# Softmax weights of the C heads turned by VectorE and DRAM instead of TensorE, with the convolution's taps spread over more steps, in a one-layer hybrid decoder block

## The chip, the cores and the metric

One core of a Trainium2 chip runs the whole program. The metric is the device time of one execution in microseconds (us), and of several executions the median. A profiled execution is one more execution, recorded by the hardware profiler. Its times in the trace count from the start of its span. Engines are called PE (TensorE), DVE (VectorE), ACT (ScalarE), POOL (GpSimd) and SP (SyncE, which here only issues DMAs).

## The reference

One layer on 512 tokens of width 2048, in float32, cut to what matters:

```
h   = rms_norm(x)
p   = h @ W_in                       # split by columns: A q k v | B u g | C q k v
A:  8 heads x 64, dilated sliding windows (128,1), (512,4), (2048,16)
B:  glu(u, g) -> causal depthwise conv, 31 taps, 512 channels -> layer norm -> swish
C:  16 query heads x 64 on 2 k/v heads, window 128, a sink per head
        w = exp(s - m) ; o = (w @ v) / (sum(w) + exp(sink - m))
x   = x + concat(A, B, C) @ W_out
x   = x + swiglu(rms_norm(x))        # width 5632
```

Attention of a C head is banded: a block of 128 queries sees its own block of keys and the one before it. For `w @ v` on PE, w must lie with keys in the partitions, while scores and softmax leave it with queries in the partitions. So each C head's weights, 128 x 512 in four packed blocks of 128 x 128, must be transposed.

## The kernel before, in words

Everything is kept with channels in partitions and the 512 tokens as columns. Each float32 operand is split in a high and a low half that PE multiplies at full rate, and each product is three matmuls of 128 x 512 (`mm3`, L322 high by high, L323 low activations by high weights, L324 high activations by low weights). The halves of the weights are made per unit of 1024 weight columns: ACT casts `wh` (L289), DVE subtracts `wl` (L263, in the FFN L285). SP loads the raw tile `w` (L243).

The program has these stages in a row on PE: idle matmuls that bridge the first loads (L348); the first four projection blocks together (`in`, the first 12 matmuls of them at L516, from four small weight tiles); 26 more projection blocks (`project`), each 2 units of weights; 32 half blocks of the output projection (`o`, two PSUM banks by turns, each freed by the residual add at L1098 on DVE); the FFN's two big products with a seven-product scheme (`out`, L1304 to L1307 up, L1569 to L1571 down); and a short end with one turn of a leftover piece (`sides`, L1534).

The mixers A, B and C run underneath the projection's matmuls. What they issue on every engine is put in order by hand, by a clock of ticks: `ticks.after(n, fn)` runs `fn` n ticks later, and `project` ticks once for every two of its k steps, that is after every 6 matmuls. Each engine then works its instructions in that order, waiting at each for its inputs. SP's queue is in order too: a DMA that waits for its source holds back the loads behind it.

For a head of C (`head(h)` in `attention`), the steps are: `scores` (PE L843/L844, tile `c3s` for mixer c3), `pack` (DVE), `packed_exps` (ACT, tile `c0e`), `packed_norm` (DVE L870, sums and their reciprocals), then `packed_flip`: four PE transposes (L877) into a PSUM bank `c0t`. One tick later `packed_high` casts the high half (ACT L883, `c0hp`), then `packed_low` subtracts for the low half (DVE L888, `c0lp`), `spread_out` masks both for the two key blocks (POOL L897/L900, `c0ph`, `c0pl`), and `weigh` multiplies by v (PE L965/L966, `c0o`). `C_TICKS` holds the distances; its seventh entry `fl` is the ticks from `packed_norm` to the flip. `at_v` adds them up to place `weigh`.

The values v are already turned on another path (`do_v`): DVE turns 32 x 32 blocks (L747), four DMAs write them to DRAM so that the blocks change places (L753, 32 x 16 x 32 with runs of 128 bytes), and one DMA reads the result back (L759).

The convolution of B is 124 DVE operations (`tap`: 4 of form L571, 120 of form L573, each on up to 128 x 512). Tap number i of block j comes `TAP_TICKS[j]` ticks after the one before; the last falls on tick 193, and the layer norm starts by tick 246.

Of the kernel before, what the change touches and what calls it, by code (L numbers as in the profile page):

```python
# [9 lines left out]
F32 = mybir.dt.float32  # L10
# [3 lines left out]
AF = mybir.ActivationFunctionType  # L14
# [17 lines left out]

OUT_ORDER = (list(range(16)), [n + o for n in range(6) for o in (0, 8)] + [6, 7, 14, 15])

TAP_TICKS = (1.2, 1.3, 1.6, 1.6)
T_LN = 244
T_GLU = 14

# [1 line left out]
SD, KD, VD, EV = 9, 6, 12, 1  # L40


C_TICKS = (1, 6, 2, 2, 2, 3, 5, 1, 4)
A_TICKS = (0, 8, 2, 1, 3, 1, 3, 1, 5)


# [70 lines left out]
def kernel(ctx: ExitStack, tc: tile.TileContext, xT, wi, wo, wgu, wd, cst_in, outT):  # L117
# [20 lines left out]
    def slot(name, dt=F32, cols=T):  # L138
        return sp.tile([P, cols], dt, name=name, tag="s")

    def bank(name, cols=T, pool="banks"):
        return psum[pool].tile([P, cols], F32, name=name, tag="b")
# [114 lines left out]
    def lows_now():  # L257
        if lows and cooling:
            release()
            pump(RAW_EARLY if at["use"] <= 20 else RAW_BUFS)  # L260
        while lows:
            fn, *args = lows.pop(0)
            fn(*args)  # L263
        if late_lows and not cooling:
            pump(RAW_EARLY if at["use"] <= 20 else RAW_BUFS)

    def split_up_to(i):
        while at["split"] <= min(i, len(works) - 1):
            key, last, eng = works[at["split"]]
            of = [b for b, k in held.items() if k == key]  # L270
            t, n = drop(key) if last else raws[key]
            if cooling:
                held.update((b, None) for b in of)
                cool.extend(of)
            u = at["split"]
            hi = wp.tile([P, 1024], F32R, name=f"wh{u}", tag="hi", bufs=SPLIT_BUFS)
            lo = wp.tile([P, 1024], F32R, name=f"wl{u}", tag="lo", bufs=SPLIT_BUFS)
            if eng == "moves":

                near = psum["high"].tile([P, 1024], F32R, name=f"wn{u}", tag="h")  # L280
                src = t[:, :n].rearrange("p (n f c) -> p f n c", n=4, c=P)
                by = lambda x: x[:, :n].rearrange("p (f n c) -> p f n c", n=4, c=P)
                nc.scalar.copy(by(near), src)
                nc.scalar.copy(by(hi), src)
                nc.vector.tensor_sub(by(lo), src, by(near).bitcast(F32))  # L285
            elif eng or "high" not in psum:
                eng = eng or nc.vector

                (nc.vector.tensor_copy if u == 0 else nc.scalar.copy)(hi[:, :n], t[:, :n])  # L289
                lows.append((eng.tensor_sub, lo[:, :n], t[:, :n], hi[:, :n].bitcast(F32)))  # L290
                if not late_lows:
                    lows_now()
            else:
                near = psum["high"].tile([P, 1024], F32R, name=f"wn{u}", tag="h")
                nc.scalar.copy(near[:, :n], t[:, :n])
                nc.scalar.copy(hi[:, :n], t[:, :n])
                lows.append((nc.vector.tensor_sub, lo[:, :n], t[:, :n], near[:, :n].bitcast(F32)))
                if not late_lows:
                    lows_now()
            splits[u] = (hi, lo)  # L300
            at["split"] += 1
# [44 lines left out]
    b = bank("idle")  # L346
    for i in range(WARM):
        nc.tensor.matmul(b, idle, idle[:, None, :].to_broadcast([P, NT, P]), start=True, stop=True)  # L348
    b = idle = None

    nhalf = cp.tile([P, 8], F32, name="nhalf")
# [6 lines left out]
    def col(i):  # L358
        return cst[:, i:i + 1]
# [39 lines left out]

    def scaled(x, g, tag, k):  # L400
        hi, lo = slot(f"{tag}h{k}", F32R), slot(f"{tag}l{k}", F32R)
        nc.scalar.activation(hi, x, AF.Copy, scale=g)
        nc.vector.scalar_tensor_tensor(lo, x, g, hi.bitcast(F32), op0=ALU.mult, op1=ALU.subtract)
        return hi, lo

# [71 lines left out]

    g4 = [bank(f"in{j}") for j in range(HEAD4)]
    h_hl = {}
    split_up_to(0)  # L480
    h_hl[0] = scaled(xs[0], col(C_G1), "h", 0)
    split_up_to(1)
    h_hl[1] = scaled(xs[1], col(C_G1 + 1), "h", 1)
    split_up_to(2)
    pump(RAW_EARLY)
    for k in range(KT):

        if k == 1:
            split_up_to(3)
        if k + 2 < KT:  # L490
            h_hl[k + 2] = scaled(xs[k + 2], col(C_G1 + k + 2), "h", k + 2)
        if k == 0:

            at["use"] = 2
            first = [splits.pop(u) for u in range(2)]
        elif k < 4 or k % 2 == 0:
            wh, wl = next_unit()
            o = 0
        if k + X_AHEAD < KT:
            load_first(k + X_AHEAD)  # L500
        elif k + X_AHEAD == KT:

            nc.sync.dma_start(cst[:, C_G2:], cst_in[:, C_G2:])
        if k == 0:
            add_square(ssum, xs[0], 0, "sq")
        if k + 1 < KT:
            add_square(ssum, xs[k + 1], k + 1, "sq")
        hi, lo = h_hl.pop(k)
        h_hi.append(hi)
        h_lo.append(lo)  # L510
        if k == 0:

            for part, u in ((0, 0), (0, 1), (2, 0), (1, 0), (1, 1), (2, 1)):
                for j in range(2):
                    w = first[u][part == 2][:, j * P:(j + 1) * P]
                    nc.tensor.matmul(g4[2 * u + j], w, (hi, lo, hi)[part], start=part == 0, stop=False)  # L516
            first = w = None
            continue
        for j in range(HEAD4):
            mm3(g4[j], wh[:, o:o + P], wl[:, o:o + P], hi, lo, False, k == KT - 1)  # L520
            o += P
# [274 lines left out]
    def attention(kind, box, mix, mi, heads):  # L796
# [34 lines left out]
        def head(h):  # L831
# [38 lines left out]
                nc.vector.tensor_add(den, den, mx)  # L870
                invert(h, den)

            def packed_flip():
                b = bank(f"{name}t{h}")
                for i in range(NT):
                    s = slice(i * P, (i + 1) * P)
                    nc.tensor.transpose(b[:, s], es["e"][:, s], ident)  # L877
                es.clear()
                ticks.after(ev, packed_high, b)

            def packed_high(b):
                hi = slot(f"{name}hp{h}", F32R)
# [114 lines left out]
            if kind == "c":  # L997
                ticks.after(tu, packed_exps)
                ticks.after(tu + s2, packed_norm)
                ticks.after(tu + s2 + fl, packed_flip)  # L1000
            else:
                for t in range(len(TBANKS[kind])):
                    ticks.after(tu + s2 + fl + t, flip, t)
# [213 lines left out]
    def later(n, fn, *args, queue=evacs):  # L1217
        while len(queue) <= n:
            queue.append([])
        queue[n].append((fn, *args))  # L1220
# [250 lines left out]
    def turn_back(key, lo=0, hi=T):  # L1471

        g, i, k, a = key
        if (g, i, k) not in pairs_out:
            name, c = BACK[g, i, k]
            pairs_out[g, i, k] = wp.tile([P, 1024], F32, name=f"z{g}{i}{k}", tag=f"raw{final_bufs[c][name]}", bufs=1)
        z = pairs_out[g, i, k].rearrange("p (b a j) -> p a b j", a=2, j=32)[:, a, lo // 32:hi // 32]
        nc.vector.transpose(z, y[key][:, lo:hi].rearrange("p (b j) -> p b j", j=32))
        if hi == T:
            y.pop(key)  # L1480
# [10 lines left out]
    class Down:  # L1491
# [100 lines left out]
        def copy_u(self, a, b):  # L1592
            u = slot(f"d{self.t}u{a}")
            nc.scalar.copy(u, b)
            later(0, self.less, 1, 0, a, u, nc.gpsimd)

        def done(self, q, banks):
            for a, b in enumerate(banks):
                if q == 7:
                    self.add(1, 1, a, b)  # L1600
                elif q == 1:
                    self.add(0, 0, a, b)
                elif q == 4:
                    self.add(1, 0, a, b)
                elif q == 6:
                    if a:
                        later(0, self.six, a, b)
                    else:
                        self.six(a, b)
                elif q == 5:  # L1610
                    self.less(1, 1, a, b)
                    if self.end:
                        turn_back(self.sum(1, 1, a))
                        if a == 1:
                            t = y[self.sum(0, 1, a)][:, TH:]
                            nc.vector.tensor_add(t, t, b[:, TH:])
                            later(0, put, self.g, 1, 1)
                else:
                    self.add(0, q - 2, a, b)
            if self.end and q == 6:  # L1620
                for a in range(2):
                    later(a, turn_back, self.sum(1, 0, a))
                later(2, put, self.g, 1, 0, queue=extras)
            if q == 3 and self.final:
                for n, (i, k) in enumerate(((0, 0), (1, 1), (1, 0), (0, 1))):
                    for a in range(2):
                        later((2, 3, 6, 7)[n] + a, turn_back, self.sum(i, k, a))
                    later((4, 5, 8, 9)[n], put, self.g, i, k, queue=extras)
# [90 lines left out]
```

## Time and profile before

| | us |
|---|---|
| median of 3 runs | 1841.1 |
| the three runs | 1840.91, 1841.10, 1842.79 |
| profiled execution, its own time | 1842.92 |
| its span in the trace | 1841.2 |

The profiled execution stands 1.8 us above the median, and 1.7 us of its time lie outside its span. The granted clock of PE over the span is 1.000. To read the stages: the first four projection blocks end at about 51 us, the projection and the mixers run to about 387 us, the output projection to 578 us, and from there to the end the FFN. A page of the profile gives for each engine the busy time, a chain of work that ended last, and the idle time before groups of instructions with the engine that ended it; views of the trace give the same by window, tile or time.

### The profile page before, as it was taken

The page shows a single profiled execution, that of the slowest core. Times are in us where ns is not written, and L with a number is a line of the kernel's source. Part 1 is how long each engine was busy: PE and PEld are TensorE (multiplying, and loading weights), DVE is VectorE, ACT ScalarE, POOL GpSimd, SP SyncE. Part 2 cuts the span into 40 slices and gives each one's busy share as a digit, 9 for nine tenths or more (in the row PEclk, how much of TensorE's full clock was granted, in tenths as well). Part 3 has the DMA queues.
Part 4 walks back from the last instruction along what each step waited for, and adds up shares of the span by engine and source line. Part 5 has one row for each costly group of instructions (what it writes and reads, how often), then busy time and mean ns, then how long its engine had stood idle before and what let it go on. Part 6 is the DMA issues. An engine that isn't in the chain of part 4 may idle for free.

```text
span 1841.2 us, 26561 instructions
## 1 busy us (share of the span) xinstructions
PE 1834.3 (100%) x8314; PEld 1522.9 (83%) x8314; DVE 1429.5 (78%) x2023; ACT 1313.2 (71%) x1784; POOL 1019.3 (55%) x793
## 2 busy tenths in 40 slices
PE   9999999999999999999999999999999999999998
PEld 7888888888888888888888888888888888888887
DVE  6689888986689877778777787777777777777777
ACT  6355644553468788888888888888887778777775
POOL 0126544110003557876878767887776559776552
PEclk9999999999999999999999999999999999999999
DMA  7354245363343456777867777677687579777635
GB/s 276 87 150 119 90 133 162 110 168 130 132 139 103 115 157 186 196 206 187 226 181 208 203 190 223 176 209 210 175 272 256 202 230 300 245 260 259 238 120 109
DMA packets 401613, 337.81 MB, mean 183 GB/s; under 512 B 185409, under 2 KB 327873, under 8 KB 401473
## 3 DMA queue, kind: packets, MB, share of 16 engines
q1 hardware_dynamic: 400896, 335.33, 62.6%
q8 instruction: 66, 1.08, 0.2%
q10 hardware_dynamic: 576, 0.79, 0.1%
q14 instruction: 75, 0.61, 0.1%
HBM read 261.61 MB, written 66.03 MB: 178 GB/s over the span
## 4 chain that ended last, share of the span: by engine, by line
PE 99%; DVE 1%; DMA 0%; issue 0%; ACT 0%; SPq 0%; DVEq 0%; ACTq 0%
PE out L1307 15%; PE out L1306 15%; PE out L1304 15%; PE out L1569 7%; PE out L1570 7%; PE out L1571 7%; PE o L322 3%; PE o L324 3%; PE o L323 3%; PE cq L322 2%; PE cq L323 2%; PE cq L324 2%; PE aq L322 1%; PE ak L322 1%; PE aq L324 1%; PE av L322 1%
## 5 line engine op out<-in xcount | busy, mean ns | idle before, releaser
L1307 PE MATMUL out<-wh,h 128*128 128x512 f32 x1232 | 479.3, 389 | 0.0
L1306 PE MATMUL out<-wl,h 128*128 128x512 f32 x1232 | 479.3, 389 | 0.0
L1304 PE MATMUL out<-wh,h 128*128 128x512 f32 x1232 | 479.3, 389 | 0.0
L1306 PEld LDWEIGHTS out<-wl,h 128*128 128x128 f32 x1232 | 231.2, 188 | 48.1
L1304 PEld LDWEIGHTS out<-wh,h 128*128 128x128 f32 x1232 | 231.2, 188 | 48.0
L1307 PEld LDWEIGHTS out<-wh,h 128*128 128x128 f32 x1232 | 231.2, 188 | 47.9
L1570 PE MATMUL out<-wl,a 128*128 128x512 f32 x620 | 240.5, 388 | 0.1
L1569 PE MATMUL out<-wh,a 128*128 128x512 f32 x620 | 240.4, 388 | 0.0
L1571 PE MATMUL out<-wh,a 128*128 128x512 f32 x620 | 240.4, 388 | 0.0
L289 ACT CAST wh<-w 128x1024 fp32r<-128x1024 f32 (+2 forms) x94 | 97.0, 1031 | 139.4 <-PE o L323 49.9
L1579 DVE TENSOR_TENSOR y<-y,out 128x512 f32<-128x512 f32 x192 | 128.5, 683 | 48.1 <-PE out L1571 46.8
L263 DVE TENSOR_TENSOR wl<-w,wh 128x1024 fp32r<-128x1024 f32 (+2 forms) x95 | 114.4, 1204 | 34.8 <-ACT wh L289 34.6
L1570 PEld LDWEIGHTS out<-wl,a 128*128 128x128 f32 x620 | 116.4, 188 | 24.2 <-DVE wl L285 0.5
L1571 PEld LDWEIGHTS out<-wh,a 128*128 128x128 f32 x620 | 116.4, 188 | 23.9
L1569 PEld LDWEIGHTS out<-wh,a 128*128 128x128 f32 x620 | 116.4, 188 | 23.9
L573 DVE SCALAR_TENSOR_TENSOR y<-bu,cst,y 128x511 f32<-128x511 f32 (+14 forms) x120 | 88.8, 740 | 1.1
L322 PE MATMUL o<-mh_c,wh 128*128 128x512 f32 x128 | 51.0, 399 | 0.0
L322 PE MATMUL cq<-hh,wh 128*128 128x512 f32 x128 | 50.3, 393 | 0.0
L324 PE MATMUL o<-mh_c,wl 128*128 128x512 f32 x128 | 50.0, 391 | 0.0
L323 PE MATMUL o<-ml_c,wh 128*128 128x512 f32 x128 | 50.0, 390 | 0.0
L323 PE MATMUL cq<-hl,wh 128*128 128x512 f32 x128 | 49.9, 390 | 0.0
L324 PE MATMUL cq<-hh,wl 128*128 128x512 f32 x128 | 49.9, 390 | 0.0
(2353 smaller groups left out, 4746.8 us busy)
## 6 DMA issues: line engine op xcount, KB each, us to landing
od<-a SPq DMA_DIRECT2D x154, 256.0 KB
a<-od SPq DMA_DIRECT2D x154, 256.0 KB
w<-in_wi SPq DMA_DIRECT2D x58, 512.0 KB
w<-in_wo SPq DMA_DIRECT2D x32, 512.0 KB
x<-in_xT SPq DMA_DIRECT2D x16, 256.0 KB
xr<-in_xT SPq DMA_DIRECT2D x16, 256.0 KB
x2d<-xr SPq DMA_DIRECT2D x16, 256.0 KB
z<-x2d SPq DMA_DIRECT2D x64, 64.0 KB
```

What stands on the lines that cost most here:

```text
L263: fn(*args)
L289: (nc.vector.tensor_copy if u == 0 else nc.scalar.copy)(hi[:, :n], t[:, :n])
L322: nc.tensor.matmul(out, wh, xh, start=start, stop=False)
L323: nc.tensor.matmul(out, wh, xl, start=False, stop=False)
L324: nc.tensor.matmul(out, wl, xh, start=False, stop=stop)
L1304: nc.tensor.matmul(b, x[:, high], wh[:, s], start=c == f == 0 and q in (7, 1, 5, 2), stop=False, skip_group_check=True)
L1306: nc.tensor.matmul(b, x[:, high], wl[:, s], start=False, stop=False, skip_group_check=True)
L1307: nc.tensor.matmul(b, x[:, low], wh[:, s], start=False, stop=c == f == 1, skip_group_check=True)
L1569: nc.tensor.matmul(b[:, lo:hi], x[:, high], wh[:, s], start=start, stop=False, skip_group_check=True)
L1570: nc.tensor.matmul(b[:, lo:hi], x[:, high], wl[:, s], start=False, stop=False, skip_group_check=True)
L1571: nc.tensor.matmul(b[:, lo:hi], x[:, low], wh[:, s], start=False, stop=last, skip_group_check=True)
L1579: getattr(eng, op)(t, t, src)
```

## The change

For the C heads, `packed_flip` is gone. `packed_turn` runs right behind `packed_norm`: DVE turns the 32 x 32 blocks of the weights (`c0z`). One tick later four SP DMAs write it to DRAM (`c0ed`), two ticks later one SP DMA reads it back into SBUF (`c0et`), and four ticks after that `packed_high` and `packed_low` work from `c0et` in SBUF in place of `c0t` in PSUM. `fl` grows from 5 to 6, so that `packed_high` and all behind it, `weigh` too, comes one tick later.

The taps' distances grow, and the last tap falls on tick 224 in place of 193, 31 later. The layer norm's tick stays.

At the start there are five more small idle matmuls; the cast of the first activation tile (`hh`) is shared by ACT and DVE; the low half of the first weight units is made after the low half of that tile; and the first 12 matmuls go high-high, low-high, then high-low for all.

At the end of the FFN, the evacuation of the second bank of product 5 (`five`) is put off to the next turn of the queue of evacuations.

```diff
-TAP_TICKS = (1.2, 1.3, 1.6, 1.6)
+TAP_TICKS = (1.4, 1.5, 1.9, 1.9)
-C_TICKS = (1, 6, 2, 2, 2, 3, 5, 1, 4)
+C_TICKS = (1, 6, 2, 2, 2, 3, 6, 1, 4)
...
+    for i in range(5):
+        nc.tensor.matmul(b[:, :P], idle, idle, start=True, stop=True)
...
-        nc.scalar.activation(hi, x, AF.Copy, scale=g)
+        if k or tag != "h":
+            nc.scalar.activation(hi, x, AF.Copy, scale=g)
+        else:
+            nc.scalar.activation(hi[:, :TH], x[:, :TH], AF.Copy, scale=g)
+            nc.vector.tensor_scalar(hi[:, TH:], x[:, TH:], g, None, op0=ALU.mult)
...
+    late_lows.append(True)
     split_up_to(0)
     h_hl[0] = scaled(xs[0], col(C_G1), "h", 0)
+    lows_now()
+    late_lows.clear()
...
-            for part, u in ((0, 0), (0, 1), (2, 0), (1, 0), (1, 1), (2, 1)):
+            for part, u in ((0, 0), (0, 1), (1, 0), (1, 1), (2, 0), (2, 1)):
...
-            def packed_flip():
-                b = bank(f"{name}t{h}")
-                for i in range(NT):
-                    s = slice(i * P, (i + 1) * P)
-                    nc.tensor.transpose(b[:, s], es["e"][:, s], ident)
-                es.clear()
-                ticks.after(ev, packed_high, b)
+            def packed_turn():
+                z = slot(f"{name}z{h}")
+                nc.vector.transpose(z, es.pop("e"))
+                ticks.after(1, packed_leave, z)
+            def packed_leave(z):
+                d = tc.dram_tile([T, P], F32, name=f"{name}ed{h}")
+                for a in range(4):
+                    at = slice(32 * a, 32 * a + 32)
+                    nc.sync.dma_start(d.rearrange("(n i) c -> i n c", i=32)[:, :, at],
+                                      z[at].rearrange("p (n c) -> p n c", c=32))
+                ticks.after(2, packed_back, d)
+            def packed_back(d):
+                t = slot(f"{name}et{h}")
+                nc.sync.dma_start(t.rearrange("p (b c) -> p b c", b=NT), d.rearrange("(b p) c -> p b c", p=P))
+                ticks.after(fl + ev - 3, packed_high, t)
...
-                ticks.after(tu + s2 + fl, packed_flip)
+                ticks.after(tu + s2, packed_turn)
...
+        def five(self, a, b):
+            self.less(1, 1, a, b)
+            if self.end:
+                turn_back(self.sum(1, 1, a))
+                ...
                 elif q == 5:
-                    self.less(1, 1, a, b)
-                    if self.end:
-                        turn_back(self.sum(1, 1, a))
-                        ...
+                    if self.end and a:
+                        later(0, self.five, a, b)
+                    else:
+                        self.five(a, b)
```

Three places show how it moves instructions. The first is PE at the flip of mixer c0's head 0, between the end of projection block `cq` and the scores of c3. Before:

```order
L324 MATMUL cq_1138<-hh_479,wl_1082 128x512
L877 MATMUL c0t_1252<-ident,c0e_1120 128x128 x4
L843 MATMUL c3s_1260<-ckh_1000,cq_1014 128x256
L844 MATMUL c3s_1260<-ckl_1001,cq_1014 128x256
L843 MATMUL c3s_1260<-ckh_1000,cq_1014 128x256
L844 MATMUL c3s_1260<-ckl_1001,cq_1014 128x256
L322 MATMUL bu_1272<-hh_142,wh_1139 128x512
```

After the change:

```order
L324 MATMUL cq_1140<-hh_485,wl_1085 128x512
L852 MATMUL c3s_1264<-ckh_1004,cq_1018 128x256
L853 MATMUL c3s_1264<-ckl_1005,cq_1018 128x256
L852 MATMUL c3s_1264<-ckh_1004,cq_1018 128x256
L853 MATMUL c3s_1264<-ckl_1005,cq_1018 128x256
L322 MATMUL bu_1276<-hh_146,wh_1141 128x512
```

The transposes are gone and nothing takes their place on PE.

The second place is SP's queue around the same two heads (`w` are weight loads, `cq1d` to `cq1t` the trip of a query block's norms, `c0sums` that of the heads' sums). Before:

```order
L243 DMA w_1155<-in_wi 128x1024
L642 DMA cq1d<-cq1p 32x4x4 x4
L685 DMA cq_1133<-cq1l 64x512
L686 DMA cq_1134<-cq1l 64x512
L243 DMA w_1220<-in_wi 128x1024
L647 DMA cq1t<-cq1d 128x16
L243 DMA w_1293<-in_wi 128x1024
L816 DMA c0sums<-weights_sums_553 8x32 x4
```

After the change:

```order
L243 DMA w_1157<-in_wi 128x1024
L892 DMA c0ed_1201<-c0z_1186 32x16x32 x4
L651 DMA cq1d<-cq1p 32x4x4 x4
L694 DMA cq_1135<-cq1l 64x512
L695 DMA cq_1136<-cq1l 64x512
L243 DMA w_1229<-in_wi 128x1024
L898 DMA c0et_1244<-c0ed_1201 128x4x128
L656 DMA cq1t<-cq1d 128x16
L243 DMA w_1298<-in_wi 128x1024
L825 DMA c0sums<-weights_sums_559 8x32 x4
L892 DMA c0ed_1321<-c0z_1290 32x16x32 x4
L898 DMA c0et_1362<-c0ed_1321 128x4x128
```

Head 0's write stands ahead of the query block's trip and its read between two weight loads; head 1's write and read stand in a row behind the sums.

The third place is DVE shortly ahead of the first residual add of the output projection (`a2s` to `a2e` is a head of A, `ml_a` the low half of a mixer's output, `xr` the residual). Before:

```order
L263 TENSOR_TENSOR wl_4256<-w_3796,wh_4255 128x1024
L922 SCALAR_TENSOR_TENSOR a2e_4313,a2d_3921<-a2e_4313,mult_a 128x512
L808 RECIPROCAL weights_sums_554<-a2d_3921 128x4
L907 ISA a2s_4315,a2d_3922<-a2s_4315,bias_a 128x256
L907 ISA a2d_3922 128x1
L907 ISA a2s_4315,a2d_3922<-a2s_4315,bias_a 128x128
L907 ISA a2d_3922 128x1
L910 SCALAR_TENSOR_TENSOR a2d_3922<-a2d_3922,aq2r 128x2
L1020 TENSOR_TENSOR ml_a_4349<-mix_a_4143,mh_a_4348 128x512
L1098 TENSOR_TENSOR xr_4248<-xr_4248,o_0_4252 128x512
```

After the change:

```order
L263 TENSOR_TENSOR wl_4318<-w_3850,wh_4317 128x1024
L582 SCALAR_TENSOR_TENSOR y_3431<-bu_1464,cst,y_3431 128x487
L942 SCALAR_TENSOR_TENSOR a2e_4377,a2d_3975<-a2e_4377,mult_a 128x512
L817 RECIPROCAL weights_sums_560<-a2d_3975 128x4
L927 ISA a2s_4379,a2d_3976<-a2s_4379,bias_a 128x256
L927 ISA a2d_3976 128x1
L927 ISA a2s_4379,a2d_3976<-a2s_4379,bias_a 128x128
L927 ISA a2d_3976 128x1
L930 SCALAR_TENSOR_TENSOR a2d_3976<-a2d_3976,aq2r 128x2
L1040 TENSOR_TENSOR ml_a_4414<-mix_a_4202,mh_a_4413 128x512
L1118 TENSOR_TENSOR xr_4310<-xr_4310,o_0_4314 128x512
L582 SCALAR_TENSOR_TENSOR y_3431<-bu_1464,cst,y_3431 128x486
```

Before, all 120 taps of form L573 stand ahead of this add; after the change 115 of them (then L582) do, and taps stand among its neighbours.

More of the change, by code (lines that the diff above doesn't have):

```diff
@@ L1595, in copy_u @@
             later(0, self.less, 1, 0, a, u, nc.gpsimd)
+        def five(self, a, b):
+            self.less(1, 1, a, b)
+            if self.end:
+                turn_back(self.sum(1, 1, a))
+                if a == 1:
+                    t = y[self.sum(0, 1, a)][:, TH:]
+                    nc.vector.tensor_add(t, t, b[:, TH:])
+                    later(0, put, self.g, 1, 1)
         def done(self, q, banks):
@@ L1610, in done @@
                 elif q == 5:
-                    self.less(1, 1, a, b)
-                    if self.end:
-                        turn_back(self.sum(1, 1, a))
[L1614 to L1617, printed above, removed]
+                    if self.end and a:
+                        later(0, self.five, a, b)
+                    else:
+                        self.five(a, b)
                 else:
```

## The prediction

> **What bounds the kernel now.** I read the busy shares first, then the chain that ended last, then PE's waits, then a window that leaves out both ends.
>
> ```profile
> PE 1834.3 (100%) x8314; PEld 1522.9 (83%) x8314; DVE 1429.5 (78%) x2023; ACT 1313.2 (71%) x1784; POOL 1019.3 (55%) x793
> PE 99%; DVE 1%; DMA 0%; issue 0%; ACT 0%; SPq 0%; DVEq 0%; ACTq 0%
> PE idle L348 <- DVE nhalf L352: 1.1, 1, 1.1
> PE sides L1534 <- DVE y L1548: 0.6, 1, 0.6
> PE in L516 <- ACT hh L402: 0.5, 1, 0.5
> 10.00:1830.00 1820.00, 1820.00 (x8261) 1513.46 (x8260) 1420.08 (x2005) 1307.65 (x1774) 1017.62 (x781) 1.00 0.63 183
> ```
>
> PE is the chain, and its three waits all lie in the first 5 us or the last 10. In the window (columns: length, then busy time of PE, PE's weight loads, DVE, ACT, POOL, then granted clock) PE is busy for 1820.00 of 1820 us at clock 1.00. So time comes off only where PE has less to issue, and is added only where PE is made to wait. Every edit is costed by these two questions.
>
> **1. The transposes that PE loses.** There are 64, four for each of 16 heads.
>
> ```profile
> 50.00:330.00 280.00, 9.56 (x64) 7.93 (x64) 1.00 0.44 124
> L877 PE MATMUL c0t<-ident,c0e x8: 270/272/273, 129.6 to 139.5; 128*128 128x128 f32 x8
> 233.22 0.39 PE L324 MATMUL ak<-hh,wl 128*128 128x512 f32 x1
> 233.45 0.60 PE L877 MATMUL c7t<-ident,c7e 128*128 128x128 f32 x4
> 233.80 0.48 PE L322 MATMUL ak<-hh,wh 128*128 128x512 f32 x1
> 234.12 0.39 PE L323 MATMUL ak<-hl,wh 128*128 128x512 f32 x1
> 234.35 0.40 PE L324 MATMUL ak<-hh,wl 128*128 128x512 f32 x1
> ```
>
> The first row says that transposes cover 9.56 us of PE's time in this window. Busy times of neighbours overlap, so the cost is read from starts. Matmuls of 128x512 follow each other by 0.23 us (234.12 to 234.35). A flip takes 233.45 to 233.80, 0.35 us, and the matmul behind it 0.32 to the next start in place of 0.23: 0.67 for the two, of which 0.44 to 0.45 is the flip's (to 234.35 it is 0.90, less two starts of 0.227). Sixteen flips of 0.45 are **-7.2 us**; the ends are 16 x 0.35 = 5.6 and the 9.56 of the window. PE was the only engine with no idle time there, so all of it comes off the end.
>
> [...]
>
> **2. What takes their place.** DVE gets 16 transposes of 32x32 blocks, SP 64 writes and 16 reads, and ACT's cast and DVE's subtraction read SBUF in place of PSUM. The nearest rows are those of v's path, with the same shapes:
>
> ```profile
> L747 DVE STREAM_TRANSPOSE cvt<-cv x1: 716/716/716, 62.1 to 62.1; 128x512 f32<-128x512 f32 x1
> 348.29 1.95 SPq L753 DMA_DIRECT2D av2d<-av2t  x4
> 351.83 0.38 SPq L759 DMA_DIRECT2D av2s<-av2d  x1
> 354.57 1.74 POOL L764 TENSOR_TENSOR av2s<-av2s,n1w 128x512 f32<-128x512 f32 x1 [4.88 <-DMA av2s<-av2d]
> 124.12 0.18 DVE L808 RECIPROCAL weights_sums<-c0d 128x4 f32<-128x4 f32 x1
> 132.04 1.30 SPq L816 DMA_DIRECT2D c0sums<-weights_sums  x4
> L883 ACT CAST c0hp<-c0t x2: 587/588/589, 131.3 to 139.8; 128x512 fp32r<-128x512 f32 x2
> L883 ACT CAST c4hp<-c4t x2: 579/585/591, 270.4 to 277.0; 128x512 fp32r<-128x512 f32 x2
> 269.99 1.31 SPq L816 DMA_DIRECT2D c4sums<-weights_sums  x4
> 271.89 1.74 SPq L642 DMA_DIRECT2D cq6d<-cq6p  x4
> 274.32 0.54 SPq L686 DMA_DIRECT2D cq<-cq6l  x1
> 116.00:206.00 90.00, 90.00 (x475) 76.93 (x474) 83.18 (x176) 54.51 (x131) 49.69 (x73) 1.00 0.36 108
> 206.00:316.00 110.00, 110.00 (x552) 92.86 (x551) 90.17 (x175) 53.64 (x120) 49.93 (x88) 1.00 0.47 130
> ```
>
> The trip through DRAM takes from 348.29, the first write's issue, to 354.57, where POOL starts on the data: 6.3 us, of which 2.7 follow the read's issue. The casts of c0's two heads stood at 131.3 and 139.8 and come one tick later, six matmuls or 1.4 us: 132.7 and 141.2. For the first head DVE's turn follows its reciprocal (124.12 and 0.18) by 0.7 us, so the data are there at 125.0 + 6.3 = 131.3, 1.4 us early. For the second head SP must first send the sums (to 133.34): 139.6, 1.6 us early. Behind a late cast stand, on ACT, the `wh` casts of the weights; behind the writes and reads, on SP, the weight loads. The weights are split long before use, so a usual head costs nothing, covered by that 1.5 us; if the cover goes, it costs what it is late. The tightest is c4's second head: sums to 271.30, writes of 1.95 to 273.25, then a query block's trip that took 271.89 to 274.86, 3.0 us, so the read is issued at 276.2 and lands at 279.0, against a cast at 277.0 + 1.4: 0.6 us late. A chain of such lates, 0.6 for five of 16 heads, is the upper end, 3 us; the lower is nothing (a gain is excluded: PE did not wait there before).
>
> The DMA engines are busy 0.36 and 0.47 of the time in the two stretches (the column ahead of the last), so transfers find room.
>
> DVE gets 16 x 0.716 = 11.5 us. In the two stretches it was idle for 6.8 and 19.8 us, and half of the turns, 5.7 us, fall in each. Its subtraction for the low half now has two inputs in SBUF in place of one, which I price from
>
> ```profile
> L888 DVE TENSOR_TENSOR c0lp<-c0t,c0hp x2: 683/684/685, 135.0 to 144.6; 128x512 fp32r<-128x512 f32 x2
> L826 DVE TENSOR_TENSOR mix_c<-mix_c,c3by x1: 893/893/893, 177.9 to 177.9; 128x512 f32<-128x512 f32 x1
> ```
>
> 0.68 us with a PSUM input, 0.89 with none: up to 16 x 0.21 = 3.3 us more, half in each. So the first stretch gets 7.4 us where 6.8 are idle, before the taps that leave it, and whatever is late there the second takes up. What DVE holds back are weight halves that lie several us ahead of their use, so nothing reaches PE by my reading; it is inside the 0 to 3 us above.
>
> [...] What lateness would do is the first rival below.
>
> **3. The taps.**
>
> ```profile
> L573 DVE SCALAR_TENSOR_TENSOR y<-bu,cst,y x120: 680/728/1011, 79.7 to 360.5; 128x511 f32<-128x511 f32 x4, 128x510 f32<-128x510 f32 x4, 128x509 f32<-128x509 f32 x4, 128x508 f32<-128x508 f32 x4
> 363.00:397.00 34.00, 34.00 (x167) 28.56 (x166) 30.41 (x67) 21.52 (x37) 3.57 (x4) 1.00 0.62 162
> 397.31 0.68 DVE L1098 TENSOR_TENSOR xr<-xr,o 128x512 f32<-128x512 f32 x1
> 400.70 0.39 PE L322 MATMUL o<-mh_c,wh 128*128 128x512 f32 x1
> ```
>
> The taps' number and work stay; the last ended about 361 us and by the new order of DVE 16 come later. Eleven of these stand ahead of the first residual add at 397.31: 11 x 0.7 = 7.7 us. DVE was idle for 34 - 30.41 = 3.6 us there, so the add is up to 4.1 us late; since taps are fewer ahead of 361 us, DVE also comes there less late than before; no row tells by how much, and I take 2.4, a little over the middle of 0 to 4.1. PE takes that add's bank again at 400.70, and the add ends at 397.99: room 2.7 us. So nothing to 1.4 us. With the tight head of part 2, I take **+0.7 us** for all stalls, ends 0 and 3.
>
> **4. The start.**
>
> ```profile
> 1.12 3.59 PE L348 MATMUL idle<-idle 128*128 128x512 bf16 x8 [1.12 <-DVE nhalf L352]
> 5.20 2.08 PE L516 MATMUL in<-hh,wh 128*128 128x512 f32 x4 [0.49 <-ACT hh L402]
> 9.63 0.80 PE L516 MATMUL in<-hh,wl 128*128 128x512 f32 x2
> 10.27 0.39 PE L322 MATMUL in<-hh,wh 128*128 128x512 f32 x1
> 8.85 0.68 DVE L263 TENSOR_TENSOR wl<-w,wh 128x512 fp32r<-128x512 f32 x1
> ```
>
> The first 12 matmuls (5.20 to 10.27) start 0.42 us apart, those behind 0.23: the clock is granted in full only from about 10 us. The idle matmuls end at 4.71 and PE waits 0.49 us for `hh`. Halving the cast and five small matmuls close this gap, worth about 0.3 us at the slow pace. Whether the full clock also comes earlier I can't read from rows. If it does, the 12 matmuls end sooner and the next limit is `wl` of the second step, ready at 9.53, which the third matmul from 10.27 needs: with 0.18 us for the weight load (1522.9 us for 8314 of them on the page) it runs at 9.7 in place of 10.7 (10.27 plus two starts), 1.0 us earlier. I take **-1.0 us**, ends -0.3 and -2.6 (if the steps behind were limited by PE's pace alone: 12 starts at 0.23 in place of 0.42, plus the 0.3).
>
> [...]
>
> **5. The end.** The edit only reorders DVE work. PE's waits there, 0.6 us for `sides`, end on DVE, which was busy 12.83 of 13 us:
>
> ```profile
> 1821.00:1834.00 13.00, 12.81 (x63) 10.37 (x62) 12.83 (x20) 5.09 (x5) 0.00 (x0) 1.00 0.73 129
> ```
>
> The same work in another order ends at the same time: **0**, at best -0.6.
>
> **Sum.** 1842.92 - 7.2 - 1.0 + 0.7 + 0 = 1835.4 for an execution like the profiled one, which stood 1.8 us above the median. Carried to the median: 1841.1 - 7.5 = **1833.6 us**. A difference under 0.2%, 3.7 us, can't be told from none here, so faster begins below 1837.4 and slower above 1844.8.
>
> **Rivals.**
>
> *The trip is late for every head (slower).* If the read waits behind loads on SP, or the trip takes longer beside the weights' traffic, the cast stands on ACT and PE waits at `weigh`, 16 times. Faster ends at a lateness over the room of 1.5 us plus the slack between `c0pl` and PE's `weigh`; each microsecond beyond costs 16. To be slower than before it must eat 7.5 + 3.7 = 11.2 us, 0.7 us a head; at 0.8 a head 1833.6 + 12.8 = 1846.4. For it: SP works in order, and this row
>
> ```profile
> SPq L243 <- DVE wl L263: 16.8, 3, 6.7
> ```
>
> shows weight loads that wait up to 6.7 us on DVE between 110 and 325 us, with anything behind them. Against it: that was three times only, and heads in the new order mostly read ahead of such loads. Chance 0.07. [...]
>
> *The late taps hold the output projection's banks.* If DVE can't use its 3.6 us of idle time, which lies between steps of the A heads, nor arrives lighter, the add is 7.7 us late, less the room of 2.7: PE waits 5.0 us. Then 1833.6 - 0.7 + 5.0 = 1837.9. For it: DVE at 30.41 of 34 us. Against it: the last taps have no deadline inside a head, and heads leave DVE idle in pieces of about a tap's size. Chance 0.13, about half of it on the side of no change.
>
> *The clock's step at the start stays.* Then the start gives 0.3 and the time is 1834.3; it lies within the forecast's range and I count it there. If it goes the other way (2.6) and no stall comes, it is 1841.1 - 7.2 - 2.6 = 1831.3.
>
> *Each transpose costs PE what its row says.* 64 x 0.272 = 17.4 us, 1833.6 - 10.2 = 1823.4. The starts exclude it; chance 0.01. [...]
>
> **How the numbers follow.** Forecast 1831 to 1836: 0.76. Late taps (1836 to 1839): 0.13. Late trips: 0.07. Under 1831, by more at the start and the end: 0.04. Faster holds the first, the last and a part of the second: 0.85; same 0.08, the rest of the second and a late trip of part of the heads; slower 0.07. The range 1831.0 to 1838.5 leaves out the late trips and the low end.
>
> **What would show it.** PE's rows at c0 show scores where the flip was, and 64 fewer matmuls there; busy PE in the middle window stays whole. A wait of PE at `weigh` (c4 first) or of ACT at `c0hp` for the DMA `c0et` shows part 2 wrong; a wait of PE at `o` near 400 us for the residual add shows part 3 wrong; the matmuls' starts between 5 and 10 us show part 4. The prediction is wrong if PE's waits in the middle come to more than 4 us.

## The result, and the profile after

The changed kernel takes 1851.09 us in the median of 5 runs (1848.72 to 1853.10) against 1841.12 of before (5 runs, 1840.91 to 1842.97). The ratio is 1.0052, with a 95% interval of 1.0041 to 1.0063: slower by 8 to 12 us, where 7.5 us faster was forecast. The profiled execution is the fastest of the five, 1848.72 us with a span of 1846.7, so the trace shows a little less of the loss than the median has.

The page's busy time of the engines, the chain that ended last, PE's waits, and the middle window of the prediction:

```profile
PE 1831.2 (99%) x8255; PEld 1518.8 (82%) x8255; DVE 1440.3 (78%) x2040; ACT 1313.7 (71%) x1784; POOL 1025.0 (56%) x793
PE 88%; DVE 5%; DMA 2%; issue 2%; POOL 1%; SPq 1%; ACT 0%; DVEq 0%; POOLq 0%; ACTq 0%
PE c6o L986 <- POOL c6pl L920: 3.3, 3, 2.2
PE c4o L986 <- POOL c4pl L920: 2.3, 1, 2.3
PE c1o L986 <- POOL c1pl L920: 1.2, 1, 1.2
PE o L322 <- DVE xr L1118: 0.9, 1, 0.9
PE c6o L985 <- POOL c6ph L920: 0.4, 1, 0.4
10.00:1830.00 1820.00, 1811.84 (x8169) 1504.54 (x8168) 1425.18 (x2013) 1305.35 (x1771) 1023.39 (x781) 1.00 0.65 188
```

Before, PE was busy for all 1820 us of this window. Now it is idle for 8.2 us, and the waits name the places: `weigh` of c1, c4 and c6, each time for POOL's selects, and the first residual add. The engine count that the change meant to help, PE's busy time, did fall by 3.1 us.

The waits are not the whole loss. This is PE at c4's first head: the first `weigh` matmul, the wait, and the projection behind it. The windows below these rows have the granted clock in the third column from the right.

```profile
273.82 0.28 PE L985 MATMUL c4o<-c4ph,cv 128*128 128x256 f32 x1
276.42 0.58 PE L986 MATMUL c4o<-c4pl,cv 128*128 128x256 f32 x1 [2.32 <-POOL c4pl L920]
278.15 0.73 PE L322 MATMUL aq<-hh,wh 128*128 128x512 f32 x1
279.90 0.40 PE L323 MATMUL aq<-hl,wh 128*128 128x512 f32 x1
276.40:278.00 1.60, 1.58 (x7) 1.48 (x7) 0.48 (x1) 0.71 (x2) 0.99 (x2) 0.50 0.80 164
278.00:279.60 1.60, 1.60 (x7) 1.31 (x6) 0.75 (x1) 0.82 (x1) 0.00 (x0) 0.50 1.04 374
```

Behind the wait the clock is granted at 0.50 for 3.4 us (276.40 to 279.81). The eight matmuls of `weigh` and four of the projection take from 273.82 to 279.90, 6.1 us; at clock 1.00 they take 0.88 and 4 x 0.227, 1.8 us. So a wait of 2.3 us cost 4.3 us. At c6's second head the same happens:

```profile
326.53 0.39 PE L324 MATMUL ak<-hh,wl 128*128 128x512 f32 x1
327.29 0.39 PE L985 MATMUL c6o<-c6ph,cv 128*128 128x256 f32 x1 [0.37 <-POOL c6ph L920]
329.86 0.39 PE L986 MATMUL c6o<-c6pl,cv 128*128 128x256 f32 x1 [2.18 <-POOL c6pl L920]
331.36 0.58 PE L986 MATMUL c6o<-c6pl,cv 128*128 128x256 f32 x1 [0.77 <-POOL c6pl L920]
335.48 0.39 PE L322 MATMUL av<-hh,wh 128*128 128x512 f32 x1
331.50:333.00 1.50, 1.50 (x5) 1.32 (x6) 1.40 (x8) 0.66 (x1) 0.00 (x0) 0.50 0.83 178
```

From 326.53 to 335.48 are 8.95 us; the same pieces at clock 1.00 need 3.4 (eight matmuls of `weigh` 0.88, seven starts of 0.227, a flip 0.35, two scores 0.54). That is a loss of 5.6 us, 3.3 of it in waits.

The account, by starts in the profiled pair: c1 1.6 us (its wait of 1.2 and 0.4 around it: PE's lead falls from 3.45 us to 2.25, with a flip gained between), c4 4.3, c6 0.9 at its first head and 5.6 at its second, the output projection 1.1, together 13.5 lost. Gained: 1.5 at the start and 16 flips of 0.43 (below), 6.9. The sum is +5.1; PE's first FFN matmul comes 4.86 us later than before, so the readings are good to some 0.2 us. The rest of the span's 5.5 us is at the end.

**What made c4 and c6 late.** At c4's first head DVE's turn ended at 255.7. SP's queue then:

```profile
255.00 0.68 DVE L885 STREAM_TRANSPOSE c4z<-c4e 128x512 f32<-128x512 f32 x1
255.48 2.27 SPq L762 DMA_DIRECT2D av0d<-av0t  x4
261.47 0.38 SPq L768 DMA_DIRECT2D av0s<-av0d  x1
261.95 2.34 SPq L892 DMA_DIRECT2D c4ed<-c4z  x4
266.37 0.39 SPq L898 DMA_DIRECT2D c4et<-c4ed  x1
270.32 0.62 ACT L903 CAST c4hp<-c4et 128x512 fp32r<-128x512 f32 x1 [2.16 <-DMA c4et<-c4ed]
```

SP stood for 3.7 us (257.75 to 261.47) at v's read-back, which waits for v's own writes to land. c4's writes came behind it, from 261.95, 6.3 us after their data. From there to the cast are 8.4 us; of all this, 2.16 us reached ACT as a wait. Before, the same cast had been

```profile
270.37 0.58 ACT L883 CAST c4hp<-c4t 128x512 fp32r<-128x512 f32 x1
```

The cast stands where it stood. It is PE that came to this `weigh` earlier, at 273.82 in place of 278.21. At c4's second head POOL's order took a hand, at c6's second head a buffer:

```profile
281.45 0.20 POOL L664 TENSOR_TENSOR cq6r<-cq6t 128x8 f32<-128x8 f32 x1 [4.06 <-DMA cq6t<-cq6d]
284.06 0.40 POOL L917 TENSOR_SCALAR_AFFINE_SELECT c4ph<-c4hp 128x256 fp32r<-128x256 f32 x1
312.50 1.94 SPq L892 DMA_DIRECT2D c6ed<-c6z  x4
324.94 0.69 DVE L908 TENSOR_TENSOR c6lp<-c6et,c6hp 128x512 fp32r<-128x512 f32 x1 [5.38 <-DMA ak1l<-ak1lo]
```

The selects of c4's second head stood behind cq6's norm, which waited 4.06 us for its DMA. Before, the selects for the high half came first. PE did not wait at this head in the profiled execution. c6's data waited 6 us for SP (turn ended 306.4, writes from 312.5), and then DVE waited 5.4 us for a buffer that SP's last copies of ak1's key still read.

### The profile page after: what moved, and what is told of

Same layout as the page of the kernel before. It is cut to its first block, busy times and chain, and to the rows that moved or that the text cites. A ratio compares the mean times of both kernels' runs of the same rounds, so it can differ in the third digit from the quotient of the medians.

```text
span 1846.7 us, 26594 instructions
## 1 busy us (share of the span) xinstructions
PE 1831.2 (99%) x8255; PEld 1518.8 (82%) x8255; DVE 1440.3 (78%) x2040; ACT 1313.7 (71%) x1784; POOL 1025.0 (56%) x793
## 4 chain that ended last, share of the span: by engine, by line
PE 88%; DVE 5%; DMA 2%; issue 2%; POOL 1%; SPq 1%; ACT 0%; DVEq 0%; POOLq 0%; ACTq 0%
PE out L1324 15%; PE out L1326 15%; PE out L1327 15%; PE out L1591 7%; PE out L1589 7%; PE out L1590 7%; PE o L322 3%; PE o L323 3%; PE o L324 3%; DVE y L582 1%; PE cq L322 1%; PE cq L323 1%; PE cq L324 1%; DVE wl L263 1%; PE in L324 1%
## 5 line engine op out<-in xcount | busy, mean ns | idle before, releaser
L582 DVE SCALAR_TENSOR_TENSOR y<-bu,cst,y 128x511 f32<-128x511 f32 (+14 forms) x120 | 89.5, 746 | 0.6
```

The lines of the kernel that those rows point to most:

```text
L582: nc.vector.scalar_tensor_tensor(yconv[j][:, i:], hconv[j][:, :T - i], c, yconv[j][:, i:], op0=ALU.mult, op1=ALU.add)
```

## The experiments

For each run: how far PE was ahead (-) or behind (+) of the profiled run of before, in us, at the first matmul of `bu2` (83.71 us before; the start's part), of `av0` (240.33; eleven flips later), of the scores of a1 (337.94; all C heads done) and of the FFN (577.80), from the starts in the timelines. The ratio is to the kernel before, run beside it on the same chip. e8 and e9, which have one run each, are told below.

| run | bu2 | av0 | a1s | FFN | median us / before | ratio, 95% |
|---|---|---|---|---|---|---|
| the change | -1.49 | -4.42 | 3.76 | 4.86 | 1851.09 / 1841.12 | 1.0052 (1.0041 to 1.0063) |
| e1 turn only | -2.04 | -1.31 | 4.59 | 4.59 | 1848.40 / 1842.13 | 1.0039 (1.0026 to 1.0051) |
| e2 rest only | -2.28 | -2.30 | -2.32 | -2.32 | 1840.97 / 1842.13 | 0.9992 (0.9984 to 1.0001) |
| e3 c4, c6 on PE | -1.57 | -3.74 | -4.05 | -4.05 | 1839.32 / 1842.13 | 0.9985 (0.9976 to 0.9994) |
| e4 weigh later | -1.44 | -4.05 | 8.37 | 9.48 | 1850.91 / 1842.13 | 1.0047 (1.0035 to 1.0060) |
| e5 ACT's queue | -2.00 | -4.43 | 4.48 | 5.61 | 1847.28 / 1842.54 | 1.0034 (1.0021 to 1.0046) |
| e6 buffer reused | -1.93 | -3.13 | 5.20 | 6.34 | 1849.03 / 1842.54 | 1.0037 (1.0023 to 1.0050) |
| e7 c1, c4, c6 on PE | -2.14 | -6.00 | -4.81 | -4.81 | 1838.13 / 1842.54 | 0.9980 (0.9971 to 0.9989) |
| e10 ACT, cast early | -1.85 | -3.02 | 4.46 | 4.46 | 1848.76 / 1842.53 | 1.0035 (1.0021 to 1.0048) |
| e11 e7, c4 weigh later | -2.23 | -5.79 | -5.61 | -5.61 | 1837.53 / 1842.53 | 0.9975 (0.9965 to 0.9985) |
| e12 c6 back on DRAM | -2.24 | -5.83 | -3.73 | -3.73 | 1841.38 / 1842.62 | 0.9996 (0.9987 to 1.0005) |

### One part alone: e1 and e2

e1 is the kernel before with the turn and `fl`:

```diff
-C_TICKS = (1, 6, 2, 2, 2, 3, 5, 1, 4)
+C_TICKS = (1, 6, 2, 2, 2, 3, 6, 1, 4)
-                ticks.after(tu + s2 + fl, packed_flip)
+                ticks.after(tu + s2, packed_turn)     # and packed_leave, packed_back
```

> Only the turn of the C heads' weights by DVE and DRAM (with fl 6); taps, start and end as before. Theory A (the weights of c4's and c6's heads come too late for weigh, since SP, POOL and shared buffers stand in their way, and PE's clock falls behind each wait): the 7.2 us of flips come off, the lates of some 12 us stay or grow with the denser taps: 1846 to 1853 us, with PE waits at c4o and c6o. Theory B (the late taps hold the output projection and load DVE at the wrong time): without late taps the loss is gone: about 1834 to 1836 us.

e2 is the change with `packed_flip` and `fl` 5 put back, so the taps, the start and the end alone.

> The taps, start and end of the change, with the flips on PE as before. Theory A: the start's 1.5 us come off, the first residual add is late by 0 to 1 us: 1839.6 to 1841 us, no waits at c4o and c6o. Theory B: it keeps most of the loss: 1847 us or more.

e1 measured 1848.40 us, e2 1840.97. e1's waits of PE:

```profile
PE c6o L977 <- POOL c6pl L911: 2.4, 2, 2.2
PE c1o L977 <- POOL c1pl L911: 2.3, 1, 2.3
PE c6o L976 <- POOL c6ph L911: 1.3, 1, 1.3
PE c4o L977 <- POOL c4pl L911: 0.7, 2, 0.5
```

The turn alone makes the loss, without late taps: theory B falls. c1 waits longer than in the change (2.3 and 0.6 against 1.2 us), probably since the denser taps load DVE there: it is busy for 9.70 of the 10 us from 170, in the change for 9.36. c4's waits are shorter, where PE came 3 us later (-1.31 at `av0` against -4.42). e2 has no wait of PE between the start and the last 10 us, so the late taps alone do not hold the residual add.

### The heads of c4 and c6 on PE: e3

```diff
+        on_pe = mi in ('c4', 'c6')
+        if on_pe:
+            fl = 5
...
-                ticks.after(tu + s2, packed_turn)
+                if on_pe:
+                    ticks.after(tu + s2 + fl, packed_flip)
+                else:
+                    ticks.after(tu + s2, packed_turn)
```

> The change, but the heads of c4 and c6 (4 of 16) are flipped on PE as before. Theory A: the waits at c4o and c6o (2.3 and 3.7 us) and the slow clock behind them go, 4 x 0.45 = 1.8 us of flips come back: 1851 less 10 to 12, plus 1.8: 1839 to 1843 us; with c1's and the output projection's waits left at 1.2 and 0.9. Theory C (the extra transfers slow everything that needs DMA, weights too): three quarters of the transfers are still there, so three quarters of the loss stays: 1847 us or more.

It measured 1839.32 us. Its one wait of PE in the middle over 0.4 us:

```profile
PE c1o L997 <- POOL c1pl L931: 1.0, 1, 1.0
```

Taking 4 of 16 heads off the DRAM path turned a loss of 10 us into a gain of 2.8 (ratio 0.9985). Three quarters of the transfers are still there, so they do not slow the kernel as such; theory C falls. The residual add's wait is gone too, though the taps come as late as in the change; why was not tried.

### More time before weigh: e4

`C_TICKS` ends in 6 in place of 4.

> The change, with every C head's weigh two ticks (2.7 us) later and nothing else moved on purpose. Theory A: a wait of up to 2.7 us is covered, c4's 2.3 and c1's 1.2 go, of c6's 2.2 and 0.8 little is left: 1838 to 1843 us. Theories B and C: no more than a wait moved elsewhere, 1849 to 1853 us.

It measured 1850.91 us, and theory A in this form failed; the time lies in the range given to theories B and C, whose causes e1 and e3 exclude. The waits moved and grew:

```profile
PE a0t L961 <- DVE a0e L942: 3.3, 1, 3.3
PE c4o L986 <- POOL c4pl L920: 3.1, 1, 3.1
PE c4o L985 <- POOL c4ph L920: 2.4, 1, 2.4
```

At c4 PE was no further ahead than in the change (-4.05 at `av0`), but the turn of c4's first head ended at 263.0 in place of 255.7 and its cast came at 277.8 in place of 270.3: seven microseconds later, where `weigh` moved by 2.7. The copies of ak2 and av0's trip before it on SP had slid as well. Room at one step does not help when the chain of in-order queues before it slides too; what started the slide was not taken apart.

### Which queue, which buffer: e5, e6 and e10

e5 issues the DMAs of c4 and c6 on ACT:

```diff
+        own = nc.scalar if mi in ("c4", "c6") else nc.sync
-                    nc.sync.dma_start(d..., z[at]...)       # and the read back
+                    own.dma_start(d..., z[at]...)
```

> The change, with the five DMAs of each head of c4 and c6 issued by ACT and not by SP. Theory A1 (SP's queue: c4's write stands 6 us behind the read-back of v and the loads, though its data are there): the write starts when DVE's turn ends, the waits at c4o go and those at c6o fall by half or more; 1840 to 1845 us. Theory A2 (POOL's order and the shared buffers make them late): the waits at c4o and c6o stay within 1 us of the change's 2.3 and 3.7, 1848 to 1853 us.

It measured 1847.28 us, between the two ranges. At c4's first head the writes started at 256.2 in place of 261.95, as A1 has it. But the cast came at 269.76, only 0.56 us earlier than in the change: in ACT's order it stands behind casts of v and of a query block. The 2.3 us of wait there still went down to about 0.3, for the most part because the first two selects of the low half took 0.40 us each in place of 0.83 and 0.85. So this run does not show that SP's queue made that wait. At c6o 2.5 us of wait were left of 3.7, where A1 had half or less. And c4's second head now waited:

```profile
268.41 0.35 ACTq L893 DMA_DIRECT2D c4ed<-c4z  x1
281.31 0.62 ACT L904 CAST c4hp<-c4et 128x512 fp32r<-128x512 f32 x1 [1.63 <-issue]
279.78 1.22 POOL L664 TENSOR_TENSOR cq6r<-cq6t 128x8 f32<-128x8 f32 x1 [5.03 <-DMA cq6t<-cq6d]
287.35 0.39 PE L987 MATMUL c4o<-c4pl,cv 128*128 128x256 f32 x1 [1.93 <-POOL c4pl L921]
```

Its trip took 12.9 us, from 268.41 to the cast at 281.31: only one write went at 268.41, the other three at 273.23 and the read at 277.14, with ACT's own work between. The selects still stood behind cq6's norm.

e6 reads the data back into `c0z`'s buffer, so that each head takes one buffer less:

```diff
-                ticks.after(2, packed_back, d)
+                ticks.after(2, packed_back, d, z)
-            def packed_back(d):
-                t = slot(f"{name}et{h}")
+            def packed_back(d, t):
```

> The change, with the data read back from DRAM into the buffer of the turned weights (c0z) and not into one of its own, so that 16 fewer buffers are taken in turn. Theory A2: DVE's 5.4 us before c6lp, which waits for a buffer that ak1's DMA still reads, go, and with them PE's 2.2 and 0.8 us at c6's second head; c4's 2.3 stay: 1844 to 1848 us. Theory A1: as the change, 1849 to 1853 us.

It measured 1849.03 us, above the range of A2 and at the low end of A1's. DVE's wait before c6's low half was still there:

```profile
DVE c6lp L907 <- DMA ak1l<-ak1lo: 7.2, 1, 7.2
```

It is 7.2 us, so taking 16 fewer buffers did not remove it. The buffer that c6lp gets is the one that SP's late copies of ak1 hold. c4's 2.3 us at its first head, which were to stay, shrank to 0.3: a slow stretch behind c1's waits (183.51 to 186.92) had brought PE there some 1.3 us later (-3.13 at `av0` against -4.42), which accounts for a part of it.

e10 is e5 with `fl` 5 for c4 and c6, which puts the selects for c4's high half ahead of cq6's norm again.

> The change, with c4's and c6's DMAs issued by ACT as in an earlier run, and their casts one tick earlier (fl 5), so that POOL's order is again that of before: the selects for c4's high half ahead of cq6's norm. Theory A2a (POOL's order made c4's second head late, since the selects stood behind cq6's norm, which waits for its DMA): c4's second head waits under 1 us, so 2 to 4 us less than with ACT's queue alone: 1843 to 1846 us; c6 stays. Rival (the trip alone is too long there): the cast is late now and c4 waits as long as before, 1847 to 1850 us.

It measured 1848.76 us, and A2a failed: c4's second head waited 4.5 us in one piece. POOL had

```profile
283.08 0.92 POOL L920 TENSOR_SCALAR_AFFINE_SELECT c4ph<-c4hp 128x256 fp32r<-128x256 f32 x1 [9.01 <-DMA ak0h<-ak0hi]
285.93 0.60 POOL L664 TENSOR_TENSOR cq6r<-cq6t 128x8 f32<-128x8 f32 x1
288.48 0.41 POOL L920 TENSOR_SCALAR_AFFINE_SELECT c4pl<-c4lp 128x256 fp32r<-128x256 f32 x1
```

The first select of the high half came at 283.1, only 1.0 us earlier than in the change (284.1), since the trip took from 270.5 to 282.4, 11.9 us. The norm then stood ahead of the low half, from 285.9 to 288.5, which is 2.6 of the 4.5 us. So the late trip says when the selects can start, and POOL's order which half waits behind the norm.

### The clock behind a wait: e8 and e9

Both are the kernel before, in which POOL writes the low half's selects again for the first heads of c0, c5 and c2, to make PE wait by set amounts: 2, 3 and 4 sets in e8; 3, 5 and 7 in e9.

```diff
-                for t in range(2):
+                more = {"c0": 3, "c5": 5, "c2": 7}.get(mi, 1) if what == "pl" and h == 0 else 1
                     parts[t] = slot(f"{name}{what}{h}{t}", F32R)
+                for t in [0, 1] * more:
```

> The kernel before, with POOL's selects for the low half repeated for the first heads of c0 (once more), c5 (twice) and c2 (three times): the same values, written again. It makes PE wait at weigh by set amounts, some 0, 2 to 4 and 5 to 7 us. Theory A's part on the clock: behind each wait of about 2 us or more PE runs at half its clock for some 3 us, which costs 1.5 to 2 us besides the wait; waits under 1 us cost themselves alone. Rival: the slow matmuls behind c4's and c6's waits came from something else, and here the clock stays at 1.00.

> As the run before it with repeated selects, which left PE almost no wait (0.3 us at c0, 0.4 at c2), with more repeats: c0 three sets, c5 five, c2 seven. Waits of PE of about 2, 2 and 5 us. Theory A's part on the clock: behind a wait of about 2 us or more the matmuls go at half pace for up to 3 us, 1.5 to 2 us beyond the wait. Rival: the granted clock stays at 1.00 behind each.

e8 left PE almost no wait (0.3 us at c0), and its clock was 1.00 all along: slack at `weigh` was larger there than I had put it. e9 took 1854.67 us in its one run. Its three waits; then the 3.41 us around the first of them and the 3.41 us behind these; then the two stretches of 3.41 us that share the wait at c5:

```profile
PE c2o L968 <- POOL c2pl L902: 4.4, 1, 4.4
PE c0o L968 <- POOL c0pl L902: 2.0, 1, 2.0
PE c5o L968 <- POOL c5pl L902: 1.9, 1, 1.9
140.62:144.03 3.41, 1.44 (x10) 1.28 (x10) 3.27 (x9) 0.20 (x1) 3.41 (x9) 1.00 0.92 276
144.03:147.44 3.41, 3.41 (x10) 2.64 (x9) 2.99 (x5) 2.05 (x5) 3.17 (x9) 0.50 0.30 96
205.47:208.88 3.41, 2.35 (x15) 1.80 (x13) 3.27 (x10) 0.59 (x1) 3.41 (x8) 1.00 0.67 222
208.88:212.29 3.41, 2.53 (x14) 2.20 (x15) 2.03 (x5) 0.71 (x2) 3.25 (x9) 1.00 0.05 13
```

PE lost 4.0 us at c0 (from 1.12 ahead to 2.87 behind), 2.35 at c5 and 6.4 at c2, for waits of 2.0, 1.9 and 4.4 us. So a wait alone can bring the slow clock, in 3.4 us of it (144.03 to 147.44 behind c0, 236.19 to 239.60 behind c2), and PE then loses 2.0 us more at each. But not always: 1.9 us at c5 brought none, and a wait of 2.3 us in e12 below none either. What sets these places apart no run tested.

### Toward a better kernel: e7, e11 and e12

e7 is e3 with c1's heads on PE too.

> The change, but the heads of c1, c4 and c6 (6 of 16) flipped on PE. Theory A: c1's 1.0 us of wait goes and 0.9 us of flips come back: 1838.5 to 1840 us, without waits of PE at any c head. If c1's wait was DVE's lateness, it shows up at c5 or c2 instead.

It measured 1838.13 us, a little under the range. The wait did not go to c5 or c2. But PE, now 6.0 us ahead at `av0`, waited 1.3 us at c4's first head, where the flips are on PE as before.

e11 adds one tick to `weigh` of c4 (`we += mi == "c4"`).

> The best so far (flips on PE for c1, c4 and c6, all else changed), with weigh of c4's heads one tick (1.4 us) later. c4's wait of 1.3 us goes: 1836.5 to 1838 us. If c4's data move along with weigh (as with all heads' weigh two ticks later), the wait stays: 1838 to 1839 us.

It measured 1837.53 us, the lowest median, 5.0 us under the kernel before (ratio 0.9975); the wait at c4 fell to 0.6 us. By the medians it can't be told from e7, whose interval overlaps; the traces have it 0.8 us further ahead at the FFN.

e12 has c6 on DRAM again, through ACT's queue with the early cast, since e10 had shown no wait there beyond 0.4 us.

> Flips on PE for c1 and c4 alone (weigh of c4 one tick later), c6 by DVE and DRAM with ACT's queue and the cast a tick earlier, the rest as changed: what each earlier run left without a wait. If the causes are separate, c6 stays without a wait of over 0.5 us and the two heads' flips, 0.9 us, come off the best so far: 1836 to 1837.5 us. If c6 was free of waits in the run with ACT's queue only because PE came there some 9 us later, its wait of 2 to 4 us is back: 1839 to 1843 us.

It measured 1841.38 us, the second case:

```profile
PE c6o L1001 <- POOL c6pl L935: 2.6, 2, 2.3
320.47 0.28 PE L1000 MATMUL c6o<-c6ph,cv 128*128 128x256 f32 x1
323.01 0.39 PE L1001 MATMUL c6o<-c6pl,cv 128*128 128x256 f32 x1 [2.26 <-POOL c6pl L935]
```

In e10 PE reached this `weigh` at 331.2, after its long wait at c4, and c6's data were there at 331.8. In e12 PE is there at 320.5 and the data at 323.6. A head that looks free of waits may be so only because PE lost time ahead of it.

## Why the prediction was wrong, point by point

**The flips (-7.2 us): right, a little large.** In e7, nine flips lie off PE between `bu2` and `av0` (c0, c3, c5 and c2 with two heads each, c7 with one), and PE gains 6.00 - 2.14 = 3.86 us between them: 0.43 a flip, 6.9 for 16, against 0.45. The 272 ns a piece that the row gave, and the rival built on it, are excluded.

**The start (-1.0 us): right in size, but not what one pair shows.** The profiled pair gives -1.5. Runs without the start's edits stood at 0 (before), -2.0 (e1), -0.9 (e8) and -1.1 (e9) at `bu2`, runs with them from -1.4 to -2.3. The means differ by 0.9 us (4 runs against 10). That e2's timed runs gained about 1 us agrees, though its interval touches 1. But the sum had the gain come from an earlier full clock, and no run shows that closing the gap of 0.49 us ahead of the first matmuls brings one; so the size is in part luck. By the traces' clock records the full clock came at 10.0 us in the kernel before and at 6.7 in the change, but at 4.1 to 4.6 in e1, e8 and e9, which have the old start. The starts agree: 0.42 us apart up to 10.27 before and 0.23 behind it, in the change 0.23 from 6.92 on. With the new start PE's lead at `bu2` goes with that time, from 2.2 to 2.3 us where it came by 4.6 us (e2, e11, e12) down to 1.4 at 6.9 (e4). Between runs with the full clock by 4.6 us, the old start's lead is 1.3 in the mean and the new one's 2.25, again 0.9. In the change the steps went on without a gap:

```profile
5.18 1.90 PE L525 MATMUL in<-hh,wh 128*128 128x512 f32 x4
8.77 0.39 PE L322 MATMUL in<-hh,wh 128*128 128x512 f32 x1
```

**The stalls (+0.7 us, at most 3): the term that failed.** They were 13.5 us in the profiled pair. Four steps of it were wrong:

- The trip. I took 6.3 us from v's row for av2 and let the margin of 1.5 us cover the rest. The trip to the cast took 8.4 us at c4's first head, and 9.5 at c0's (writes from 123.46, read 129.26, cast 132.99). From the first write to the read's issue lay 4.4 and 5.8 us in place of 3.5, and from there to the cast 4.0 and 3.7 in place of 2.7.
- SP's queue. I counted what stands ahead of c4's second head, and missed that at c4's first head v's read-back stands ahead of the write and held it 6.3 us (2.16 of them a wait of ACT), and at c6's second head the sums and av1's writes, 6 us.
- POOL. That the selects are a tick later, and so come behind cq6's norm, is not in the sum. In the profiled execution it cost PE no wait; in e5 it stood ahead of one of 1.9 us.
- The clock. A wait was priced at its own length. Of the 13.5 us, 8.1 are waits; the other 5.4 lie in the matmuls around them, 4.3 of it at the two stretches of half clock (2.0 at c4, 2.3 at c6).

**The turns' load on DVE: as priced or less.** The turns took 0.67 to 0.71 us each, and the low half's subtraction stayed at 0.68 to 0.69 us for seven of eight mixers with both inputs in SBUF; the 0.21 us that I added did not come (c7 alone took 0.89 to 0.93).

**The taps: right.** The first residual add held PE for 0.9 us, inside 0 to 1.4. The rival with 5 us did not come. In e2 and e3, with the same taps, the add held PE for nothing, so the late taps alone do not make this wait.

**The end: no gain,** as said; the last stretch came out up to 0.7 us longer in the change, and between -0.2 and +1.0 us in the other runs, with and without the edit, so no effect can be told.

**The rivals.** The late trip was the right one in kind and went to the right side, with a chance of 0.07. Its place was wrong: it is not every head but c4 and c6. c1's wait is not of this kind: ACT did not wait there for the data, and POOL began the selects for its first low half at 180.8 in place of 181.0 before; PE came 2.5 us earlier. By e3 the four heads of c4 and c6 do better with their transposes on PE (1839.32 us against 1851.09); the ten that e7 and e11 leave on the path through DRAM do not need it (1838.13 and 1837.53 us against 1842.5 of before).

The step behind all four: I looked for room between the data and their use where PE stood before. But PE came to c4 nearly six microseconds earlier than before (4.4, with `weigh` a tick later), and its partners' chain (SP, DVE, ACT, POOL) did not. Before, c4's second head already had next to none to spare: POOL's last select for it ended at 289.05, and `weigh` ran to 289.4. Each microsecond saved on PE ahead of it was one taken from that room.

## What to carry to other kernels

Moving work off the bound engine shortens its time only up to the next place where it meets another engine's chain; so check the slack of every later meeting, less the gain so far, not the slack of the moved step alone. A path through an in-order DMA queue is priced with the longest wait that may stand ahead of it there (6.3 us from c4's data to their first write), and a wait of the matmul engine with the slow clock that can follow it (3.4 us at 0.50, some 2 us beyond the wait). Moving only the heads with slack (10 of 16, with c4's `weigh` a tick later) gave 5 us, some 1 of it at the start, where moving all lost 10.

## What the runs showed of the hardware

A wait of PE of 2.0 to 4.4 us was followed by 3.41 us at half clock at four places in the change and in e9, and by none at two others, in e9 and e12:

| run and place | PE's wait, us | PE idle in the 3.41 us ahead of the slow stretch, us | granted clock |
|---|---|---|---|
| the change, c4's first head | 2.32 | 2.30 | 0.50 from 276.40 to 279.81 |
| the change, c6's second head | 2.18 and 0.77 | 2.60 | 0.50 from 331.01 to 334.42 |
| e9, c0 | 1.97 | 1.97 | 0.50 from 144.03 to 147.44 |
| e9, c2 | 4.37 | 2.80 | 0.50 from 236.19 to 239.60 |
| e9, c5 | 1.95 | no slow stretch | 1.00 from 205.47 to 212.29 |
| e12, c6 | 2.26 | no slow stretch | 1.00 from 320 to 327 |

So the length of the wait alone did not decide here: 1.97 us at c0 was followed by the slow clock, 2.26 in e12 was not. Nor did the slow stretch always begin where the wait ended: at c0 in e9 it began 1.4 us later (142.64, then 144.03), at c4 in the change with it (276.42, 276.40). What sets these places apart was not shown. In the slow stretch behind c0 the matmuls of 128x512 started 0.43 us apart (144.24 to 146.80), behind it 0.23.

With both inputs in SBUF DVE's subtraction for the low half took 0.68 to 0.69 us for seven mixers and 0.89 to 0.93 for c7 (the change), and POOL's select of 128x256 took 0.83 to 0.85 us at the low half of c4's first head in the change and 0.40 at the same place in e5; what decides was not measured.
